# Storing three branches' gated terms apart and adding them in the last merge on VectorE

## Chip, cores and metric

The kernel runs on one core of one Trainium2 chip. The metric is device time in microseconds (us) of one execution; lower is better. Engines are named as in the profile: PE is TensorE (PEld its weight loads), DVE is VectorE, ACT is ScalarE, POOL is GpSimd, and SP (SyncE) issues most of the transfers.

## Reference

The program is a layer with four attention-like branches followed by a second block. The part that matters here is the merge of the four branches:

```python
branches = ((y_a, a_z), (y_b, b_z), (y_c, c_z), (y_d, d_z))
merged = None
for i, (y, z) in enumerate(branches):
    yi = y.reshape(B, S, BRANCH_W) * jax.nn.silu(z)
    term = jax.nn.sigmoid(h @ w_merge[i]) * (yi @ w_br[i])
    merged = term if merged is None else merged + term
return x + gate * (merged @ w_out)
```

With S = D = 1024 and BRANCH_W = 256, each term is a 1024 x 1024 matrix: a gate product of 1024 inner columns, a branch product of 256, and a sum of four such terms. Everything is in float32.

## The kernel before

All large products are computed transposed, in tiles of 128 x 512 (128 output columns of the model, 512 tokens, a "half"). A float32 product is three products of high and low halves (`mm3`, lines 229 to 231), so a gate tile is 24 matmuls of 512 columns and a branch tile is 6. `load_w` loads weights and splits them into a high half (ACT, or DVE at line 149) and a low half (line 155 on POOL or line 157 on DVE, in turn).

`merge(bi, y, step)` is called four times: step 0 for branch d, step 1 for branch a, step 2 for branch c, step 3 for branch b. Each has four groups of four tiles, 16 tiles in all. A group is put on the list `fillers` and issued by `fill`, which the attention loops of the next branch call between their tiles: step 1 runs beside branch c, step 2 beside branch b, step 3 after branch b's last tiles. In each step the running sum of the earlier steps lies in DRAM (`acc_d`), is loaded into `acc` (line 1134), gets the step's term added on POOL (line 1150) and is stored (line 1157); step 0 only stores, and step 3 keeps the result: ACT and DVE split it into `gT`, the left operand of the product with `w_out`.

The gate `tanh(x/2)` of six of the groups of `w_merge` is computed early, by `pre`, and stored in DRAM (`pre_d`): all four groups of branch a and two of branch c. For these, `w is None`, and the gate is loaded into `tz` (line 1137). Otherwise the tile computes it on PE and ACT (line 1142). The line that makes the term reads the gate and the PSUM bank of the branch product on DVE (line 1149): (gate + 1) x product. That instruction is what frees the bank. There are two banks with the tag `mm`, which gate products and branch products share in turn.

Buffers set the order of the work: `acc` and `tz` have two buffers each, `Pm` (tiles of 128 x 1024 in which the branches hold probabilities) has three, and weights have nine (`w`). A Tile scheduler orders the instructions of each engine by a simulated timeline, so a change of one instruction can move others. Every engine works through its own queue in order, SP's too: a transfer whose buffer is not free holds back those behind it.

Branch c (stick breaking) works per head: two sigmoids on ACT (lines 1101, 1102), two mask selects on POOL (line 1104), a scan on DVE (line 1106), a multiplication (line 1108) which alternates between DVE and POOL, transposes on PE (line 276), a split into high and low halves (`PT`, ACT and line 157 on DVE) and the product with the values on PE (line 816). Branch b is a banded softmax (`softmax_pair`, lines 838 to 860), whose results `y.put` and `gate` turn into the operand `y` of step 3.

Of the kernel before, what the change touches and what calls it, by code (L numbers as in the profile page):

```python
# [9 lines left out]
F32 = mybir.dt.float32  # L10
F32R = mybir.dt.float32r
AF = mybir.ActivationFunctionType
ALU = mybir.AluOpType
# [4 lines left out]
P = 128  # L18
# [58 lines left out]
def hybrid_then_mix_kernel(ctx: ExitStack, tc, I, c1, c2, out, dbg=None, upto=99):  # L77
    nc = tc.nc
    ve, ac, po, pe, sy = nc.vector, nc.scalar, nc.gpsimd, nc.tensor, nc.sync
# [7 lines left out]
    cur = [main]  # L87

    def nm(s):
        uid[0] += 1  # L90
        return f"{s}_{uid[0]}"
# [4 lines left out]
    def tmp(tag, n, bufs=2, dt=F32):  # L96
        return cur[0].tile([P, n], dt, name=nm(tag), tag=tag, bufs=bufs)
# [7 lines left out]
    def mmb():  # L105
        return bank("mm", _T["MM"])
# [77 lines left out]
    def load_w(srcs, n, kc=KC, per=None, tag="w", bufs=None, hieng=None, loeng=None, dma=None, order=None):  # L184

        per = per or min(kc, 1024 // n)
        w = W()
        w.h, w.l, w.per = {}, {}, per
        raws = []
        order = order or range(kc // per)  # L190
        for i, b in enumerate(order):
            raw = main.tile([P, per, n], F32, name=nm("wr"), tag=tag, bufs=bufs or NW)
            for src, c0 in srcs:
                (dma or sy).dma_start(raw[:, :, c0:c0 + src.shape[2]], src[:, b * per:(b + 1) * per, :])
            raws.append((b, raw))
            if len(raws) == _T["SG"] or i == len(order) - 1:
                split_w(w, raws, per, n, tag, bufs, hieng, loeng)
                raws = []
        w.hi = lambda k, c0, c1: w.h[k // per][:, k % per, c0:c1]
        w.lo = lambda k, c0, c1: w.l[k // per][:, k % per, c0:c1]  # L200
        return w

    def kview(ap):
        return ap.rearrange("(k p) n -> p k n", p=P)
# [59 lines left out]
    def gemm_T(dst, w, c0, a, half, ks=None):  # L264

        return mm3(dst, [(w.hi(k, c0, c0 + P), w.lo(k, c0, c0 + P), a.hi(k, half), a.lo(k, half))
                         for k in (ks or range(a.nk))])
# [232 lines left out]
    for kp in range(4):  # L500
# [18 lines left out]
        for q in range(4):  # L519
            w, c = first_w[q // 2], q % 2 * P  # L520
# [551 lines left out]
    def branch_c():  # L1072
# [20 lines left out]
        def tile_of(p, i, ops):  # L1093
# [3 lines left out]
            for hh in range(2):  # L1097
# [16 lines left out]
    acc_d = [[[dram.tile([P, 512], F32, name=f"acc{b}_{m}_{q}", tag=f"acc{b}_{m}_{q}", bufs=1) for q in range(2)]  # L1114
              for m in range(KC)] for b in range(3)]
    gT = A()

    def merge(bi, y, step):
        wm = kview(I["w_merge"][0, bi])
        wb = kview(I["w_br"][0, bi])  # L1120
        wbr = [None]

        def group(g):
            w = None
            if (bi, 2 * g, 0) not in pre_d:
                w = load_w([(wm[:, :, g * 256:(g + 1) * 256], 0)], 256)
            if g % 2 == 0:
                wbr[0] = load_w([(wb[:, :, g * 256:(g + 2) * 256], 0)], 512, kc=2, tag="w")
            for half in range(2):
                for m in range(2):  # L1130
                    k = 2 * g + m
                    acc = tmp("acc", 512)
                    if step:
                        sy.dma_start(acc[:], acc_d[step - 1][k][half][:])
                    t = tmp("tz", 512)
                    if w is None:
                        sy.dma_start(t[:], pre_d[bi, k, half][:])
                    else:
                        gp = mmb()
                        gemm_T(gp[:], w, m * P, hT, half)  # L1140
                        with stream(_T["STE"], -10000000):
                            ac.activation(t[:], gp[:], AF.Tanh, scale=0.5)
                    bp = mmb()
                    gemm_T(bp[:], wbr[0], (g % 2) * 256 + m * P, y, half)
                    with stream(_T["STE"], -10000000):
                        if step == 0:
                            ve.scalar_tensor_tensor(out=acc[:], in0=t[:], scalar=1.0, in1=bp[:], op0=ALU.add, op1=ALU.mult)
                        else:
                            ve.scalar_tensor_tensor(out=t[:], in0=t[:], scalar=1.0, in1=bp[:], op0=ALU.add, op1=ALU.mult)  # L1149
                            po.tensor_tensor(acc[:], t[:], acc[:], op=ALU.add)  # L1150
                        if step == 3:
                            if m == 0:
                                gT.alloc(half, g)
                            copy(gT.hi(k, half), acc[:], "a", 0.5)
                            sub_lo(gT.lo(k, half), acc[:], gT.hi(k, half), "v", 0.5)
                        else:
                            sy.dma_start(acc_d[step][k][half][:], acc[:])
        for g in range(4):
            fillers.append(lambda g=g: group(g))
# [185 lines left out]
    for m in range(2):  # L1345
        u, w, evac = conf_group(m)
# [21 lines left out]
    qk0, w, evac = qk_group(0)  # L1368
# [367 lines left out]
    for g in LED:  # L1736
# [4 lines left out]
        w = load_w([(w_up[:, :, g * P:(g + 1) * P], 0)], P)  # L1741
# [171 lines left out]
    acc = [ot(1024, 8, "acc") for _ in range(NT)]  # L1913
# [69 lines left out]
    for stage in range(2):  # L1983
        ts = {}
        for i, (sn, tn) in enumerate(order):
# [5 lines left out]
            for q in range(4):  # L1991
# [18 lines left out]
                if (stage, i, q) in tails:  # L2010
                    t = tails[stage, i, q]
# [93 lines left out]
```

## Time and profile before

| | |
|---|---|
| time, median of 3 runs | 2323.44 us (2321.71 to 2327.45) |
| the profiled execution's own time | 2326.04 us |
| its span in the trace | 2324.3 us |
| mean granted clock of PE | 0.989 |
| PE busy | 2235.5 us, 96% |
| DVE busy | 1518.4 us, 65% |
| ACT busy | 962.6 us, 41% |
| POOL busy | 495.1 us, 21% |

The trace is one execution. Busy time is the union of an engine's instructions; what stands in square brackets behind an instruction is the idle time of its engine just before it and whom it waited for. Matmuls are pipelined, so one takes longer than its share of the time. The granted clock is given as a share of PE's full 2.4 GHz; 0.5 is the lower level, 1.2 GHz.

### The profile page before, as it was taken

What the parts mean: (1) busy time and instruction counts of PE and PEld (TensorE: products, weight loads), DVE (VectorE), ACT (ScalarE), POOL (GpSimd) and SP (SyncE); (2) the same over time, 40 slices, a digit from 0 to 9 for tenths busy, and PEclk for the clock granted to TensorE, in tenths of its full rate; (3) what the DMA queues carried; (4) which work ended last, traced back from release to release, by engine and by line L of the source; (5) the groups of instructions that cost most, each with busy time, mean ns of one, the idle gap of its engine ahead of it and who ended that gap; (6) DMA issues with size and microseconds to landing.
All of it is one profiled execution on the core that took longest, in us unless ns stands there. A gap on an engine that the chain in (4) does not pass through costs nothing.

```text
span 2324.3 us, 30295 instructions
## 1 busy us (share of the span) xinstructions
PE 2235.5 (96%) x11004; PEld 1853.1 (80%) x11004; DVE 1518.4 (65%) x2952; ACT 962.6 (41%) x1937; POOL 495.1 (21%) x411
## 2 busy tenths in 40 slices
PE   7999999999989999999998998899999999999998
PEld 6788788888887778877887787677788888888877
DVE  7634466665677965634579876855576778678684
ACT  6211344444455544422322344634445454334452
POOL 4222100010155622224320000012043440000021
PEclk9999999999999999999999999999999999999999
DMA  9432221121132333224320211156555687524313
GB/s 326 154 95 63 60 69 50 49 88 60 33 109 85 115 121 105 73 82 147 107 68 26 82 54 34 37 172 206 161 186 187 197 324 252 181 91 155 117 55 118
DMA packets 202783, 272.72 MB, mean 117 GB/s; under 512 B 17086, under 2 KB 126214, under 8 KB 202634
## 3 DMA queue, kind: packets, MB, share of 16 engines
q1 hardware_dynamic: 194240, 257.95, 34.3%
q10 hardware_dynamic: 8394, 12.84, 1.8%
q8 instruction: 87, 1.43, 0.3%
q14 instruction: 62, 0.51, 0.1%
HBM read 199.43 MB, written 71.32 MB: 116 GB/s over the span
## 4 chain that ended last, share of the span: by engine, by line
PE 46%; DVE 6%; DMA 2%; ACT 1%; issue 1%; POOL 0%; SPq 0%; DVEq 0%; POOLq 0%; ACTq 0%
PE mm L230 6%; PE mm L231 6%; PE mm L229 6%; DVE blk L1334 2%; PE s L1676 2%; PE s L1675 2%; PE s L1674 2%; PE t L2020 1%; PE t L2021 1%; PE t L2019 1%; PE t L276 1%; PE mm L2020 1%; PE t L1676 1%; PE t L1675 1%; PE t L1674 1%; PE mm L2021 1%
## 5 line engine op out<-in xcount | busy, mean ns | idle before, releaser
L229 PE MATMUL mm<-blk,wh 128*128 128x512 f32 x1264 | 506.4, 401 | 12.7 <-DVE tz L1149 5.3
L230 PE MATMUL mm<-blk,wh 128*128 128x512 f32 x1264 | 502.1, 397 | 0.9 <-DVE blk L157 0.9
L231 PE MATMUL mm<-blk,wl 128*128 128x512 f32 x1264 | 501.0, 397 | 2.0 <-POOL wl L155 1.7
L229 PEld LDWEIGHTS mm<-blk,wh 128*128 128x128 f32 x1264 | 239.4, 189 | 65.1 <-DVE tz L1149 7.9
L231 PEld LDWEIGHTS mm<-blk,wl 128*128 128x128 f32 x1264 | 239.4, 189 | 52.4 <-POOL wl L155 2.1
L230 PEld LDWEIGHTS mm<-blk,wh 128*128 128x128 f32 x1264 | 239.5, 189 | 47.8 <-DVE blk L157 1.3
L155 POOL TENSOR_TENSOR wl<-wr,wh 128x1024 fp32r<-128x1024 f32 (+1 forms) x50 | 122.9, 2458 | 480.1 <-ACT wh L147 290.2
L229 PE MATMUL mm<-wh,blk 128*128 128x512 f32 (+3 forms) x544 | 197.0, 364 | 7.1 <-DVE wh L149 1.6
L231 PE MATMUL mm<-wh,blk 128*128 128x512 f32 (+3 forms) x544 | 194.3, 359 | 1.0 <-DVE blk L157 1.0
L157 DVE SCALAR_TENSOR_TENSOR wh<-blk,wh 128x1024 fp32r<-128x1024 f32 x116 | 138.6, 1221 | 66.9 <-issue 59.2
L147 ACT ACTIVATE wh<-blk 128x1024 fp32r<-128x1024 f32 x116 | 117.0, 1053 | 154.4 <-PE s L2020 84.5
L230 PE MATMUL mm<-wl,blk 128*128 128x512 f32 (+3 forms) x480 | 170.2, 355 | 9.5 <-DVE wl L157 9.1
L147 ACT ACTIVATE blk<-mm 64x512 fp32r<-64x512 f32 (+3 forms) x138 | 77.9, 569 | 172.0 <-PE mm L231 113.2
L147 ACT ACTIVATE PT<-t 128x512 fp32r<-128x512 f32 (+3 forms) x224 | 96.0, 460 | 118.2 <-PE o L816 65.9
L147 ACT ACTIVATE wh<-wr 128x1024 fp32r<-128x1024 f32 (+2 forms) x91 | 93.7, 1031 | 102.2 <-DMA wr<-in_w_in_dram 21.9
L157 DVE SCALAR_TENSOR_TENSOR PT<-t,PT 128x512 fp32r<-128x512 f32 (+3 forms) x224 | 111.0, 515 | 37.4 <-ACT PT L147 36.4
L309 POOL TENSOR_TENSOR sm<-sm,mhalf 128x1 f32<-128x1 f32 x64 | 38.8, 610 | 437.3 <-DVE sm L308 422.0
L229 PEld LDWEIGHTS mm<-wh,blk 128*128 128x128 f32 x544 | 103.3, 190 | 25.4 <-DVE wh L149 2.4
L231 PEld LDWEIGHTS mm<-wh,blk 128*128 128x128 f32 x544 | 103.4, 190 | 16.8 <-DVE blk L157 1.9
L230 PEld LDWEIGHTS mm<-wl,blk 128*128 128x128 f32 x480 | 91.7, 191 | 24.3 <-DVE wl L157 11.3
L157 DVE SCALAR_TENSOR_TENSOR wl<-wr,wh 128x1024 fp32r<-128x1024 f32 (+2 forms) x69 | 88.5, 1283 | 31.5 <-PE mm L230 14.0
L1150 POOL TENSOR_TENSOR acc<-tz,acc 128x512 f32<-128x512 f32 x48 | 67.8, 1416 | 132.2 <-DVE tz L1149 86.4
(364 smaller groups left out, 4851.5 us busy)
## 6 DMA issues: line engine op xcount, KB each, us to landing
acc<-acc SPq DMA_DIRECT2D x96, 256.0 KB, 2.6
wr<-in_w_merge_dram SPq DMA_DIRECT2D x32, 512.0 KB, 4.0
wu<-in_w_up_dram SPq DMA_DIRECT2D x32, 512.0 KB, 5.1
blk<-in_w_down_dram SPq DMA_DIRECT2D x32, 512.0 KB, 7.0
blk<-ss SPq DMA_DIRECT2D x32, 512.0 KB, 4.7
wr<-in_w_in_dram SPq DMA_DIRECT2D x27, 512.0 KB, 4.2
ss<-us SPq DMA_DIRECT2D x48, 256.0 KB, 2.3
blk<-sa SPq DMA_DIRECT2D x24, 512.0 KB, 4.3
```

Of the source, the lines that this page charges most:

```text
L147: return ac.activation(dst, src, AF.Copy, scale=1.0 if scale is None else scale)
L155: return po.tensor_tensor(lo, x, hi.bitcast(F32), op=ALU.subtract)
L157: return ve.scalar_tensor_tensor(out=lo, in0=x, scalar=scale, in1=hi.bitcast(F32), op0=ALU.mult, op1=ALU.subtract)
L229: pe.matmul(dst, sh, mh, start=(i == 0), stop=False)
L230: pe.matmul(dst, sh, ml, start=False, stop=False)
L231: last = pe.matmul(dst, sl, mh, start=False, stop=(i == n - 1))
L1150: po.tensor_tensor(acc[:], t[:], acc[:], op=ALU.add)
L1334: ve.scalar_tensor_tensor(out=acc[:, c:c1], in0=u[:, c - l:c1 - l], scalar=w, in1=acc[:, c:c1], op0=ALU.mult, op1=ALU.add)
L1674: pe.matmul(dst, wh, xh, start=first and k == 0, stop=False, skip_group_check=True)
L1675: pe.matmul(dst, wh, xl, start=False, stop=False, skip_group_check=True)
L1676: last = pe.matmul(dst, wl, xh, start=False, stop=k == 3, skip_group_check=True)
L2020: pe.matmul(d, sh[:, c, ts_], tl[:, c, :], start=False, stop=False)
```

## The change

Steps 0 to 2 no longer add anything: each stores its own term in `acc_d[step]`. Step 3 loads the three stored terms of a tile, the first two into the halves of one `Pm` buffer and the third into `acc`, adds them with two additions on DVE, and adds its own term with a third, also on DVE (POOL added before). In steps 1 and 2, a gate that was computed early is loaded straight into `acc` and multiplied there, so that `tz` isn't used. The number of transfers is the same: 48 loads and 48 stores of `acc_d`, but all loads now stand in step 3.

```diff
--- before.py
+++ after.py
@@ -1130,9 +1130,14 @@
                 for m in range(2):
                     k = 2 * g + m
                     acc = tmp("acc", 512)
-                    if step:
-                        sy.dma_start(acc[:], acc_d[step - 1][k][half][:])
-                    t = tmp("tz", 512)
+                    if step == 3:
+                        two = cur[0].tile([P, 1024], F32, name=nm("Pm"), tag="Pm", bufs=_T["PM"])
+                        for j in range(2):
+                            sy.dma_start(two[:, j * 512:(j + 1) * 512], acc_d[j][k][half][:])
+                        sy.dma_start(acc[:], acc_d[2][k][half][:])
+                        ve.tensor_tensor(two[:, :512], two[:, :512], two[:, 512:], op=ALU.add)
+                        ve.tensor_tensor(acc[:], two[:, :512], acc[:], op=ALU.add)
+                    t = acc if w is None and step < 3 else tmp("tz", 512)
                     if w is None:
                         sy.dma_start(t[:], pre_d[bi, k, half][:])
                     else:
@@ -1143,11 +1148,10 @@
                     bp = mmb()
                     gemm_T(bp[:], wbr[0], (g % 2) * 256 + m * P, y, half)
                     with stream(_T["STE"], -10000000):
-                        if step == 0:
-                            ve.scalar_tensor_tensor(out=acc[:], in0=t[:], scalar=1.0, in1=bp[:], op0=ALU.add, op1=ALU.mult)
-                        else:
-                            ve.scalar_tensor_tensor(out=t[:], in0=t[:], scalar=1.0, in1=bp[:], op0=ALU.add, op1=ALU.mult)
-                            po.tensor_tensor(acc[:], t[:], acc[:], op=ALU.add)
+                        x_ = t if step == 3 else acc
+                        ve.scalar_tensor_tensor(out=x_[:], in0=t[:], scalar=1.0, in1=bp[:], op0=ALU.add, op1=ALU.mult)
+                        if step == 3:
+                            ve.tensor_tensor(acc[:], t[:], acc[:], op=ALU.add)
                         if step == 3:
                             if m == 0:
                                 gT.alloc(half, g)
```

The order of the instructions moves with it. On POOL, in step 1 beside branch c (`wl` is a weight's low half, `Pm` a probability tile), there stood before:

```order
L155 TENSOR_TENSOR wl_7106<-wr_7099,wh_7105 128x1024
L1150 TENSOR_TENSOR acc_6647<-tz_6649,acc_6647 128x512
L155 TENSOR_TENSOR wl_7449<-wr_7446,wh_7448 128x1024
L1150 TENSOR_TENSOR acc_6661<-tz_6663,acc_6661 128x512
L1104 AFFINE_SELECT Pm_6797<-Pm_6797 128x128
L1150 TENSOR_TENSOR acc_6675<-tz_6677,acc_6675 128x512
L1104 AFFINE_SELECT Pm_6839<-Pm_6839 128x128
L1104 AFFINE_SELECT Pm_6840<-Pm_6840 128x128
L1108 TENSOR_TENSOR Pm_6840<-Pm_6840,Pm_6839 128x767
L1150 TENSOR_TENSOR acc_6689<-tz_6691,acc_6689 128x512
L1150 TENSOR_TENSOR acc_6703<-tz_6705,acc_6703 128x512
L1104 AFFINE_SELECT Pm_6877<-Pm_6877 128x128
```

And now, at the same place:

```order
L155 TENSOR_TENSOR wl_7082<-wr_7075,wh_7081 128x1024
L155 TENSOR_TENSOR wl_7425<-wr_7422,wh_7424 128x1024
L1104 AFFINE_SELECT Pm_6773<-Pm_6773 128x128
L1104 AFFINE_SELECT Pm_6815<-Pm_6815 128x128
L1104 AFFINE_SELECT Pm_6816<-Pm_6816 128x128
L1108 TENSOR_TENSOR Pm_6816<-Pm_6816,Pm_6815 128x767
L1104 AFFINE_SELECT Pm_6853<-Pm_6853 128x128
```

The additions are gone from between the selects and the multiplications; nothing took their place. On DVE, where branch b's last attention tile meets step 3's first tiles (L856, L858 and L150 are the tile's softmax, L826 and L827 join its output, PT is its transposed probabilities), before:

```order
L157 SCALAR_TENSOR_TENSOR PT_9397<-t_9394,PT_9397 128x2x128 [waits Activation_49]
L847 TENSOR_TENSOR sm_9421<-mx_9409,c_63 128x2 [waits DVE_49]
L856 TENSOR_TENSOR sm_9423<-sm_9423,sm_9426 128x2 [waits Activation_49]
L858 RECIPROCAL sm_9430<-sm_9423 128x2 [waits DVE_49]
L150 TENSOR_SCALAR Pm_9410<-Pm_9410,sm_9430 128x256 [waits DVE_49]
L150 TENSOR_SCALAR Pm_9415<-Pm_9415,sm_9430 128x256
L1149 SCALAR_TENSOR_TENSOR tz_9756<-tz_9756,mm_9783 128x512 [waits PE_49,Activation_49]
```

Now, with two additions and their waits for transfers ahead of the softmax, and more behind it:

```order
L1138 TENSOR_TENSOR Pm_9625<-Pm_9625 128x512 [waits DMAHW3_49,DMAHW2_49]
L1139 TENSOR_TENSOR acc_9624<-Pm_9625,acc_9624 128x512 [waits DMAHW4_49,DVE_49]
L856 TENSOR_TENSOR sm_9343<-sm_9343,sm_9346 128x2 [waits Activation_49]
L1154 TENSOR_TENSOR acc_9624<-tz_9631,acc_9624 128x512 [waits DVE_49]
L858 RECIPROCAL sm_9350<-sm_9343 128x2 [waits DVE_49]
L150 TENSOR_SCALAR Pm_9330<-Pm_9330,sm_9350 128x256 [waits DVE_49]
L150 TENSOR_SCALAR Pm_9335<-Pm_9335,sm_9350 128x256
L157 SCALAR_TENSOR_TENSOR blk_9668<-acc_9624,blk_9667 128x512 [waits Activation_49]
L826 TENSOR_REDUCE blk_8759<-o_9280 64x128 [waits Activation_49]
L1138 TENSOR_TENSOR Pm_9672<-Pm_9672 128x512 [waits DMAHW5_49,DMAHW4_49]
L1152 SCALAR_TENSOR_TENSOR tz_9678<-tz_9678,mm_9705 128x512 [waits PE_49]
```

The additions of a tile (L1138, L1139) stand well ahead of its gated product (L1152), among branch b's instructions; each waits for transfers. On SP, at the same place, there stands now (the waits for PE are for transposes out of branch b's `Pm` tiles):

```order
L194 DMA wr_9808<-in_w_merge_dram 128x4x256 [waits DMAHW5_49,DVE_49]
L194 DMA wr_9810<-in_w_merge_dram 128x4x256 [waits PE_49]
L1136 DMA Pm_9625<-acc_0_0_730 128x512 [waits DVE_49,PE_49]
L1136 DMA Pm_9625<-acc_0_0_746 128x512 [waits DMAHW3_49]
L1136 DMA Pm_9672<-acc_1_0_732 128x512 [waits DMAHW4_49,DMAHW3_49,DVE_49]
L1136 DMA Pm_9672<-acc_1_0_748 128x512
L1137 DMA acc_9716<-acc_0_1_763 128x512 [waits DVE_49]
L1136 DMA Pm_9717<-acc_0_1_731 128x512 [waits DMAHW7_49,PE_49]
```

The loads of the stored terms come in pairs into `Pm`, where before one load of the running sum stood for each tile.

On PE the products keep their number; the order shifts by some matmuls against branch b's last tile. Between that tile's transposes and its last product stood four matmuls of a gate product and three of a branch product; now all 24 of a gate product and three of a branch product stand there.

## Rows read from the trace of the kernel before

**Rows 1.** Page, busy time of each engine (us, share of the span, instructions)

```profile
PE 2235.5 (96%) x11004; PEld 1853.1 (80%) x11004; DVE 1518.4 (65%) x2952; ACT 962.6 (41%) x1937; POOL 495.1 (21%) x411
```

**Rows 2.** Engines' busy time by stage: us, then busy (instructions), granted clock, DMA share, GB/s

```profile
660.00:870.00 210.00, 191.23 (x988) 158.42 (x988) 161.91 (x252) 105.24 (x240) 106.01 (x93) 0.98 0.36 111
970.00:990.00 20.00, 19.09 (x92) 15.55 (x91) 11.67 (x24) 6.82 (x19) 5.41 (x3) 1.00 0.13 39
990.00:1080.00 90.00, 87.67 (x374) 70.84 (x373) 27.27 (x33) 22.94 (x33) 27.42 (x18) 0.98 0.30 92
1080.00:1100.00 20.00, 15.38 (x64) 11.57 (x63) 12.62 (x8) 3.37 (x5) 10.74 (x5) 1.00 0.66 234
```

**Rows 3.** Timeline of PE, matmuls that waited: start, us, what [idle before <-releaser]

```profile
681.77 0.63 PE L276 MATMUL t<-c,Pm 128*128 128x128 f32 x4 [1.63 <-DVE PT L157]
692.13 1.06 PE L816 MATMUL o<-PT,cst 128*128 128x256 f32 x4 [2.09 <-DVE PT L157]
753.37 0.55 PE L276 MATMUL t<-c,Pm 128*128 128x128 f32 x3 [1.88 <-DVE Pm L1108]
```

**Rows 4.** Waits of PE, 660 to 1100 us: total us, times, longest

```profile
PE mm L229 <- DVE tz L1149: 5.3, 7, 1.5
PE mm L231 <- POOL wl L155: 1.7, 1, 1.7
```

**Rows 5.** Timeline of POOL and DVE around those waits

```profile
678.92 1.77 DVE L1108 TENSOR_TENSOR Pm<-Pm,Pm 128x639 f32<-128x639 f32 x1
768.73 0.81 DVE L1108 TENSOR_TENSOR Pm<-Pm,Pm 128x639 f32<-128x639 f32 x1
...
685.68 2.58 POOL L1150 TENSOR_TENSOR acc<-tz,acc 128x512 f32<-128x512 f32 x2
688.20 2.29 POOL L1104 TENSOR_SCALAR_AFFINE_SELECT Pm<-Pm 128x128 f32<-128x128 f32 x2
688.64 1.76 DVE L1106 TENSOR_TENSOR_SCAN Pm<-Pm 128x768 f32<-128x768 f32 x1 [0.19 <-POOL Pm L1104]
...
751.01 1.90 POOL L1150 TENSOR_TENSOR acc<-tz,acc 128x512 f32<-128x512 f32 x1
751.95 1.37 DVE L1108 TENSOR_TENSOR Pm<-Pm,Pm 128x383 f32<-128x383 f32 x1
```

**Rows 6.** Windows of 10 us in which the granted clock fell

```profile
690.00:700.00 10.00, 7.91 (x34) 6.70 (x34) 8.98 (x11) 4.86 (x11) 6.70 (x6) 0.83 0.54 167
750.00:760.00 10.00, 7.38 (x27) 5.37 (x26) 9.59 (x14) 4.16 (x10) 9.37 (x11) 0.69 0.65 191
1020.00:1030.00 10.00, 8.29 (x30) 5.99 (x29) 3.72 (x3) 2.06 (x3) 3.77 (x3) 0.84 0.52 165
```

**Rows 7.** Page and groups by shape: adds of 128x512 on POOL and on DVE

```profile
L1150 POOL TENSOR_TENSOR acc<-tz,acc 128x512 f32<-128x512 f32 x48 | 67.8, 1416 | 132.2 <-DVE tz L1149 86.4
...
L1833 DVE TENSOR_TENSOR blk<-us,blk 128x512 f32<-128x512 f32 x10 | 14.4, 1438 | 3.5 <-ACT us L147 3.5
L1937 DVE TENSOR_TENSOR acc<-run,acc 128x512 f32<-128x512 f32 x12 | 7.8, 688 | 0.0
```

**Rows 8.** Timeline of PE and DVE at the entry of the last merge

```profile
971.00 0.60 PE L276 MATMUL t<-c,Pm 128*128 128x128 f32 x4
974.32 0.16 DVE L856 TENSOR_TENSOR sm<-sm,sm 128x2 f32<-128x2 f32 x1 [1.53 <-ACT sm L855]
979.74 0.60 PE L276 MATMUL t<-c,Pm 128*128 128x128 f32 x4
981.80 0.64 PE L816 MATMUL o<-PT,blk 128*128 128x256 f32 x4
986.36 2.65 DVE L157 SCALAR_TENSOR_TENSOR blk<-blk,blk 128x512 fp32r<-128x512 f32 x1 [0.15 <-ACT blk L147]
```

**Rows 9.** Source line 1134 (loads of the running sum), DMA to landing, last row

```profile
DMA to landing us min/median/max: 2.5/2.8/3.6
```

**Rows 10.** Timeline of POOL inside the last merge

```profile
1061.83 1.29 POOL L1150 TENSOR_TENSOR acc<-tz,acc 128x512 f32<-128x512 f32 x1 [9.65 <-DMA acc<-acc]
```

## Prediction

> **What bounds the kernel now.** I read the page first: PE is busy 96% of the span [rows 1], so a change pays only where PE waits, or where a wait goes away together with the slow clock behind it. The engines' busy time by stage shows where the merges meet such waits. Step 0 of the merge lies before 480 us and has none; steps 1 and 2 run from 670 to 970 us, step 3 from 966 to 1080. From 660 to 870 us, while branch c computes, PE works 191.23 of 210 us, so 18.8 us are idle, with DVE at 161.91 and POOL at 106.01 us. From 870 to 970 us PE is full. At the entry of step 3 it loses 0.9 us (19.09 of 20), in the body 2.3 (87.67 of 90), and in the 20 us behind it 4.6 (15.38) [rows 2]. The granted clock fell in three windows: 10 us at 0.83 and at 0.69 inside branch c, and at 0.84 inside step 3, which cost 1.7, 3.1 and 1.6 us; each has a PE wait in it or just ahead of it [rows 6]. So the change can reach at most 18.8 + 1.7 + 3.1 = 23.6 us in steps 1 and 2, and 2.3 + 1.6 = 3.9 us in the body of step 3.
>
> **Part A: steps 1 and 2 lose the add on POOL and the load of the running sum.** Of the 48 adds at 1416 ns on POOL [rows 7], 32 stand here. They sit in POOL's queue between branch c's mask selects (L1104) and half of its multiplications (L1108); the order above shows them gone. The waits of PE show what that costs. At 681.77 PE waited 1.63 us for DVE, whose multiplication L1108 of 640 columns had taken 1.77 us, against 0.81 for the same shape at 768.73 [rows 3, 5]: 0.96 us lost. At 692.13 it waited 2.09 us: a scan (L1106) had started at 688.64, after a select at 688.20 that was queued on POOL behind two adds of 2.58 us [rows 3, 5]; I take back one add, 1.3 us. At 753.37 it waited 1.88 us for an L1108 of 1.37 us that started at 751.95, while an add held POOL until 752.91 [rows 3, 5]: 0.96 us. Together 3.2 us.
>
> These rows show a DVE operation on two SBUF tiles growing by the time that a POOL add still runs. The Trainium skill (SBUF — State Buffer, Who interferes with whom) says that a VectorE instruction with two SBUF inputs and a GpSimd instruction that reads SBUF exclude each other, and that the second to issue is blocked until the first ends. By that rule the same holds for the new adds on DVE, so it speaks against the change in step 3 as much as for it here; by itself it would not change the sum, because POOL keeps only weight splits in step 3.
>
> Seven more waits, 5.3 us, are for the gated product's own instruction (L1149) [rows 4], which frees PE's bank late. Its gate now has a buffer that holds a load and a store; the old accumulator's buffer held a load, the add and a store. One step of the ring drops out and none is new, so a loss here is excluded; I take half, 2.6 us. Both clock dips here follow waits of PE; I take half of 4.8 us, 2.4. The sum is 8.2 us. DVE stays busy for 77% of the stretch and works in order, so some waits will reappear behind other instructions: I take 6 us of the 8.2. **A = -6**, bounds 0 (every wait returns elsewhere) and -12 (half of 23.6).
>
> The load that is left out, 256 KB landing in 2.8 us [rows 9], is worth nothing by itself: only POOL waited for it, and POOL's wait is already in A.
>
> **Part B: the entry of step 3.** Here the change adds a wait. The first two terms go into a buffer that branch b's last attention tiles still use (`Pm`, three buffers), and the sum of them is in DVE's order ahead of the last tile's softmax. By the rows of before: the transposes that free the first buffer ran at 971.00 for 0.60; two DMA issues (0.3 us each) and 2.8 to land give about 975.0; two adds of 0.69 end at 976.4. The instruction behind them (L856) started at 974.32 [rows 8, 9]: 2.1 us later, and 2.8 with the third add that stands there too. The next pair is loaded after the last tile's transposes (979.74) and stands ahead of the lower halves (L157) of the transposed probabilities, which that tile's last product on PE needs: transposes, loads and the adds there give some 5.6 us more. So that product (981.80) comes about 8.4 us later. What hides it: PE has a gate product of 24 matmuls and three more between those transposes and that product, 27 x 0.234 = 6.3 us (0.234 from 87.67 us over 374 matmuls [rows 2]), where it had seven, 1.6 us; the cover grows by 4.7 us. That leaves 3.7 us. After it, the branch's last lower half (986.36, 2.65 us [rows 8]) stands behind a weight split and one more add, some 1.9 us, and PE already lost 0.9 us there. The sum is 5.6 us, but the loads may land before the softmax is due, and the gate product can run on meanwhile; I take **B = +4**. The bounds are 0 (all behind PE's gate products) and +8, to which a clock dip like that at 1020 (1.6) may add itself.
>
> **Part C: the body of step 3.** 48 adds move to or are new on DVE. Each takes 688 ns when POOL is quiet and 1438 ns when POOL adds beside it [rows 7], so 33 to 69 us; I take 33, since POOL is nearly empty here. DVE has 90 - 27.27 = 62.7 us free [rows 2], and a tile is 30 matmuls, 7.0 us, against 3 x 0.69 for its adds: hidden. If that cover were gone, the 33 us would be on the path. The wait on the running sum changes engine: POOL once sat 9.65 us for that load [rows 10], and now DVE would. Queued behind it on DVE is the gated product of the current tile, which frees PE's bank; PE needs the bank only 24 matmuls (5.6 us) later. Against this the step between the product and ACT's copy shortens by 1416 - 688 = 0.7 us, so the buffer for the next load and the group's weights behind it in SP's order come sooner, which should shrink the 1.7 us wait for a weight half (L155) [rows 4] and the clock dip after it. **C = -1**, bounds -3.9 and +3. The transfers grow by 32 x 256 KB, 8.4 MB over about 100 us or 84 GB/s, on top of 92; the stage behind moved 234 GB/s [rows 2], so I cost them at nothing.
>
> **Part D: the exit.** In the 4.6 us that PE loses behind step 3, DVE is splitting w_out; its last add, 0.69, stands among those splits: **D = +0.7**, bounds 0 and +1.4.
>
> **Sum.** -6 + 4 - 1 + 0.7 = -2.3 us. The profiled execution took 2326.04 us (span 2324.3 and 1.7 around it), so 2323.7 in its own time. It lies 2.6 us above the median of 2323.44, inside the three runs' spread of 5.7 us; on the median the sum gives 2321.1, and I say 2321.
>
> **The rivals.** *Nothing is given back* (faster): the entry is hidden and A comes whole, -8 to -12, with C at -1 to -3; 2310 to 2315. For it: DVE is at 9.6 of 10 us in the window at 750 [rows 6], so each freed microsecond there counts, and the clock dips may vanish whole. Against: the entry's order. *DVE blocks at the entry* (slower): the two loads ahead of the softmax make PE wait the full 8 us plus 1.6 of clock, and A brings less than 3; 2329 to 2333. It decides if the loads of the second pair land after the 6.3 us of cover. For it: the DVE order; against: PE's longer cover. *The waits only move* (no change): branch c's DVE, at 77%, sets its pace whichever engine adds; A and B both within 1, so 2322 to 2324. *The adds lock POOL's splits out*: eight splits (L155) of the 18 POOL instructions of the body would each wait for an add, 0.69 us; only the one for which PE waits counts, with its dip up to 3; 2324. This exclusion is the rule of the Trainium skill (SBUF — State Buffer, Who interferes with whom) cited in part A.
>
> **How the numbers follow.** Chances: the forecast 0.42, nothing given back 0.27, blocked at the entry 0.17, waits only move 0.09, splits locked out 0.05. About 0.3%, 7 us, is what a measurement of this kernel tells from no change. Faster than 2316.5 are the second case and a little of the first: 0.29. Slower than 2330.4 is most of the third: 0.15. The rest, 0.56, is within. The forecast's own range is 2316 to 2327; the range that reaches into the neighbours is 2311 to 2331.
>
> **What would show it.** Right: from 660 to 870 us of the same work PE's idle time falls from 18.8 to 11 to 14 us, the mean L1108 on DVE gets shorter, and the window clock of 0.69 is gone or milder; at the entry DVE waits on a load of `Pm` or `acc` (L1138, L1139), and PE idles 3 to 6 us within 25 us; in the body no PE wait on L1152 above 1 us. Wrong: no wait of PE at the entry (then B is 0 and the time is near 2316 or below), or PE's idle time in branch c unchanged (A is 0, then 2325 or above), or adds on DVE nearer 1.4 us than 0.69 and PE waiting for L1152 in the body.

## The result

The changed kernel takes 2346.45 us (median of 4 runs, 2341.58 to 2352.42) against 2323.16 for the kernel before: a ratio of 1.0099, 95% interval 1.0082 to 1.0116, so about 23 us slower. The forecast was 2321, in a range up to 2331, with a chance of 0.15 for slower. The time lies outside that range, on the slower side.

### The profile page after: what moved, and what is told of

The parts are those of the page before. It is cut to its first block, busy times and chain, and to the rows that moved or that the text cites. A ratio compares the mean times of both kernels' runs of the same rounds, so it can differ in the third digit from the quotient of the medians.

```text
span 2342.5 us, 30253 instructions
## 1 busy us (share of the span) xinstructions
PE 2243.0 (96%) x11004; PEld 1858.8 (79%) x11004; DVE 1538.6 (66%) x3000; ACT 961.0 (41%) x1937; POOL 422.0 (18%) x363
## 4 chain that ended last, share of the span: by engine, by line
PE 78%; DVE 10%; DMA 4%; ACT 2%; issue 1%; POOL 1%; SPq 0%; DVEq 0%; POOLq 0%; ACTq 0%
PE mm L229 15%; PE mm L230 14%; PE mm L231 14%; PE t L276 3%; PE o L816 3%; DVE blk L1338 3%; PE s L1678 2%; PE s L1680 2%; PE s L1679 2%; PE t L2024 1%; PE t L2025 1%; PE t L2023 1%; PE mm L2024 1%; PE t L1678 1%; PE t L1680 1%
## 5 line engine op out<-in xcount | busy, mean ns | idle before, releaser
L229 PE MATMUL mm<-blk,wh 128*128 128x512 f32 x1264 | 508.6, 403 | 27.7 <-DVE acc L1152 12.3
L229 PEld LDWEIGHTS mm<-wh,blk 128*128 128x128 f32 x544 | 104.5, 193 | 23.8 <-DVE blk L149 2.1
L816 PE MATMUL o<-PT,blk 128*128 128x256 f32 x508 | 88.4, 295 | 2.5 <-DVE PT L157 2.4
```

The lines of the kernel that those rows point to most:

```text
L229: pe.matmul(dst, sh, mh, start=(i == 0), stop=False)
L816: behind_pe[0] = pe.matmul(dst, v(lo + c0 + j), PT[:, j].rearrange("p a q -> p (a q)"), start=start and c0 + j == 0, stop=stop and c0 + j ...
```

## The profile after

The page's busy times of the changed kernel, which answer to [rows 1]:

```profile
PE 2243.0 (96%) x11004; PEld 1858.8 (79%) x11004; DVE 1538.6 (66%) x3000; ACT 961.0 (41%) x1937; POOL 422.0 (18%) x363
```

POOL lost 73 us and DVE gained 20, as planned; PE's busy time grew by 7.5 us with the same number of matmuls, and the mean granted clock went from 0.989 to 0.986, so part of the loss is slower clock. Its profiled execution spans 2342.5 us, 18.2 more than before; the medians differ by 23, so some 5 us of the loss don't show in this pair of executions.

To see where the 18.2 went, I count matmuls. The windows view tells how many have started up to a time; both kernels have 11004. The windows begin at 0, so they give the moment at which the 3600th, 4950th and 5700th has started: near the beginning of step 1, just ahead of step 3, and behind its exit (between those ends the order differs, so a count there is a rough guide). The kernel before:

```profile
0.00:675.58 675.58, 656.94 (x3600) 558.16 (x3601) 393.14 (x1106) 274.14 (x628) 132.86 (x121) 0.99 0.29 93
0.00:960.91 960.91, 925.80 (x4950) 780.83 (x4951) 598.19 (x1513) 414.69 (x976) 254.33 (x223) 0.99 0.31 99
0.00:1138.80 1138.80, 1095.83 (x5700) 918.08 (x5700) 675.79 (x1632) 466.08 (x1082) 313.77 (x265) 0.99 0.31 100
```

The changed kernel:

```profile
0.00:674.46 674.46, 654.52 (x3600) 556.45 (x3601) 392.25 (x1106) 274.02 (x628) 131.00 (x120) 0.99 0.29 93
0.00:969.95 969.95, 926.17 (x4950) 781.76 (x4950) 591.13 (x1515) 413.92 (x977) 201.98 (x191) 0.99 0.28 89
0.00:1158.50 1158.50, 1101.94 (x5700) 921.38 (x5701) 696.64 (x1680) 465.20 (x1082) 241.47 (x217) 0.98 0.31 98
```

Steps 1 and 2 took 295.5 us instead of 285.3, so 10.2 were lost where 6 were to be gained; PE's idle time in them rose from 16.5 to 23.8. Step 3 with its exit took 188.6 instead of 177.9, a loss of 10.7 where 3.7 was forecast. The program's start (-1.1) and the rest (-1.5) make up the difference to 18.2.

The waits of PE from 640 to 1140 us of the changed kernel (total, times, longest) tell which instructions were late; these are the three largest. L1152 is now the gated product (L1149 in [rows 4]):

```profile
PE mm L229 <- DVE acc L1152: 12.3, 11, 2.9
PE mm L229 <- ACT blk L147: 4.7, 2, 4.0
PE s L797 <- DVE blk L157: 4.7, 2, 2.8
```

Seven waits for the product, 5.3 us, have become eleven of 12.3. The first two places below explain the first two rows.

**The ring of buffers.** The queue of SP from 640 to 970 us waits, among others, for these two things (L1142 loads a ready gate, L1161 stores a term):

```profile
SPq L1161 <- DVE acc L1152: 71.1, 16, 11.4
SPq L1142 <- DMA acc<-acc: 45.4, 19, 5.0
```

19 of the 24 gate loads wait for a transfer, the store of a term. The timeline shows one such turn, SP, DVE and PE together (start, duration):

```profile
759.03 0.67 DVE L1152 SCALAR_TENSOR_TENSOR acc<-acc,mm 128x512 f32<-128x512 f32 x1
759.99 0.42 SPq L1161 DMA_DIRECT2D acc<-acc  x1
763.28 0.32 SPq L1142 DMA_DIRECT2D acc<-pre  x1
768.54 0.69 DVE L1152 SCALAR_TENSOR_TENSOR acc<-acc,mm 128x512 f32<-128x512 f32 x1 [2.23 <-DMA acc<-pre]
769.28 0.50 PE L229 MATMUL mm<-blk,wh 128*128 128x512 f32 x1 [2.93 <-DVE acc L1152]
```

The product of 759.03 is stored at 759.99. The next gate can go into that buffer only when the store has landed, so its load is issued at 763.28, and the product that needs it starts at 768.54, with PE idle for 2.93 us. (This load is also the slowest of its kind, 5.2 us from issue to landing; the median of L1142 is 2.9.) Before, the gate's buffer came free when POOL had added it, and the store of the sum held another buffer. SP waited nearly as long for that store, but with the load of the running sum, which only POOL reads:

```profile
SPq L1134 <- DMA acc<-acc: 39.3, 26, 3.9
```

**The entry of step 3.** By the same count, these are the stretches from the 5000th to the 5150th matmul (the entry), on to the 5450th (the body) and on to the 5500th (the exit), of the kernel before and then of the changed one:

```profile
971.12:1005.00 33.88, 32.97 (x153) 26.97 (x152) 15.49 (x29) 10.86 (x25) 9.26 (x6) 1.00 0.23 71
1005.00:1078.41 73.41, 71.08 (x302) 57.26 (x301) 21.49 (x24) 17.82 (x26) 22.84 (x14) 0.98 0.27 84
1078.41:1095.41 17.00, 12.38 (x52) 9.15 (x51) 13.74 (x8) 4.45 (x7) 11.48 (x5) 1.00 0.83 295
979.93:1020.12 40.19, 36.16 (x152) 28.57 (x151) 28.07 (x45) 10.51 (x24) 4.05 (x2) 0.92 0.53 164
1020.12:1096.86 76.74, 72.06 (x302) 56.95 (x300) 39.21 (x52) 18.24 (x27) 8.24 (x4) 0.98 0.40 128
1096.86:1115.15 18.29, 14.22 (x52) 10.22 (x51) 10.53 (x9) 3.51 (x6) 12.62 (x5) 0.91 0.81 284
```

The entry takes 6.3 us longer, the body 3.3 and the exit 1.3. In the entry PE idles 3.1 us more and is busy 3.2 us longer, at a mean clock of 0.92. DVE, POOL, ACT and PE in the order of time:

```profile
994.36 2.41 POOL L155 TENSOR_TENSOR wl<-wr,wh 128x1024 fp32r<-128x1024 f32 x1 [29.48 <-PE mm L231]
994.41 0.41 DVE L826 TENSOR_REDUCE blk<-o 64x128 f32<-64x256 f32 x1
995.12 2.20 DVE L1138 TENSOR_TENSOR Pm<-Pm 128x512 f32<-128x512 f32 x1 [0.30 <-DMA Pm<-acc]
997.34 0.42 DVE L826 TENSOR_REDUCE blk<-o 64x128 f32<-64x256 f32 x1
997.79 0.69 DVE L1139 TENSOR_TENSOR acc<-Pm,acc 128x512 f32<-128x512 f32 x1
998.40 0.29 DVE L827 TENSOR_TENSOR blk<-blk,ju 128x128 f32<-128x128 f32 x1
998.77 1.64 POOL L620 TENSOR_TENSOR blk<-blk,tz 128x512 f32<-128x512 f32 x1 [2.00 <-DVE blk L827]
1000.44 0.63 ACT L147 ACTIVATE blk<-blk 128x512 fp32r<-128x512 f32 x1 [5.32 <-POOL blk L620]
1001.12 1.42 PE L229 MATMUL mm<-blk,wh 128*128 128x512 f32 x2 [4.03 <-ACT blk L147]
```

On DVE one addition of a later tile stands between the two reductions (L826) that join branch b's output, and another between them and the last instruction of the join (L827). The first took 2.20 us instead of 0.69, beside a weight split on POOL. POOL's gate (L620) and ACT's copy follow, and step 3's first products of that half need the copy. PE waits 4.03 us. The windows, which answer to [rows 6] and [rows 2], show the clock at this stall and at those of the body:

```profile
1000.00:1010.00 10.00, 8.88 (x27) 6.47 (x28) 6.65 (x9) 3.52 (x5) 0.41 (x1) 0.69 0.50 158
1060.00:1070.00 10.00, 7.00 (x25) 4.76 (x24) 5.66 (x7) 2.06 (x3) 1.75 (x1) 0.88 0.55 184
```

**The body of step 3.** The waits of DVE, then of ACT, from 990 to 1120 us:

```profile
DVE acc L1139 <- DMA acc<-acc: 20.1, 10, 2.9
DVE Pm L1138 <- DMA Pm<-acc: 14.2, 10, 2.2
```

```profile
ACT blk L147 <- DVE acc L1154: 46.7, 12, 7.3
```

A late load holds back DVE, where the gated product and weight splits stand behind the sums, and ACT, where the copy of the sum stands ahead of the next tile's tanh. (ACT waited before too, 34.7 us in 11 waits, for POOL's sum.) PE then waits for each:

```profile
1062.07 0.69 DVE L1139 TENSOR_TENSOR acc<-Pm,acc 128x512 f32<-128x512 f32 x1 [2.84 <-DMA acc<-acc]
1063.41 0.50 PE L229 MATMUL mm<-blk,wh 128*128 128x512 f32 x1 [0.65 <-DVE tz L1152]
1064.18 0.63 ACT L147 ACTIVATE blk<-acc 128x512 fp32r<-128x512 f32 x1 [7.24 <-DVE acc L1154]
1066.30 0.50 PE L229 MATMUL mm<-blk,wh 128*128 128x512 f32 x1 [1.22 <-ACT tz L1147]
1066.29 0.69 DVE L1138 TENSOR_TENSOR Pm<-Pm 128x512 f32<-128x512 f32 x1 [2.20 <-DMA Pm<-acc]
1068.17 0.79 PE L231 MATMUL mm<-blk,wl 128*128 128x512 f32 x1 [1.14 <-DVE wl L157]
```

These three waits of PE make 3.0 us within 5; in the whole body its idle time grew by 2.4. The clock fell there (the window from 1060 at 0.88 costs 1.2 us), but it had fallen once in the body before as well [rows 6], and its mean over the body is the same. In the exit PE idles no longer than before (4.1 us against 4.6), but its clock is 0.91 against 1.00, and why it fell there isn't shown.

## The experiments

The theory after the result has two causes that add up: the ring of two buffers in steps 1 and 2, and waits for loads at the wrong place of DVE's order in step 3. The rivals are the scheduler's new order alone, the `Pm` buffers, and the engine that adds. The table gives each kernel's median and ratio to the kernel before on the same chip, and by its profile the time that each part took more than before (start to matmul 3600, steps 1 and 2 to 4950, step 3 and exit to 5700, the rest).

| kernel | us | ratio (95%) | start | steps 1, 2 | step 3 | rest |
|---|---|---|---|---|---|---|
| changed | 2346.45 | 1.0099 (1.0082 to 1.0116) | -1.1 | +10.2 | +10.7 | -1.5 |
| e1_own_gate | 2331.39 | 1.0034 (1.0022 to 1.0045) | -4.6 | -3.6 | +13.2 | +0.3 |
| e2_ring4 | 2331.33 | 1.0031 (1.0020 to 1.0042) | +1.0 | -4.0 | +9.2 | -0.8 |
| e5_first_only | 2334.45 | 1.0046 (1.0031 to 1.0060) | -1.0 | +9.0 | -2.9 | +1.2 |
| e6_last_only | 2334.65 | 1.0048 (1.0033 to 1.0064) | -2.2 | +0.3 | +7.2 | +0.7 |
| e8_late_sum | 2335.83 | 1.0043 (1.0028 to 1.0058) | -1.2 | +10.0 | -2.5 | +3.4 |
| e3_pool_sum | 2344.22 | 1.0088 (1.0071 to 1.0106) | -2.5 | +12.4 | +5.9 | +1.6 |
| e9_own_late | 2314.75 | 0.9958 (0.9943 to 0.9973) | -3.0 | -1.9 | +0.1 | -7.9 |
| e9_again | 2317.06 | 0.9968 (0.9957 to 0.9979) | +0.1 | -1.6 | -0.3 | -8.4 |
| e10_two_in_3 | 2319.88 | 0.9984 (0.9973 to 0.9994) | +2.0 | -2.4 | -0.2 | -0.3 |
| e7_dve_chain | 2323.29 | 0.9992 (0.9981 to 1.0004) | +2.8 | +7.8 | -5.1 | -3.0 |
| e11_sum_in_2 | 2341.85 | 1.0073 (1.0058 to 1.0088) | +0.6 | +9.2 | -1.3 | +2.8 |

The start varies between -4.6 and +2.8 us; no edit touches it, and the kernel that ran twice has -3.0 and +0.1. The four parts come from one execution of each kernel. Those of e7_dve_chain (2328.70 us) and e10_two_in_3 (2325.17) took some 5 us more than their medians, that of e11_sum_in_2 (2337.30) some 5 less, so a part of 2 or 3 us that stands in one profile alone says little.

### The two parts apart

```diff
 e5_first_only (against the change)
                     if step == 3:
-                        two = ...
-                        for j in range(2): sy.dma_start(two[...], acc_d[j][k][half][:])
                         sy.dma_start(acc[:], acc_d[2][k][half][:])
-                        ve.tensor_tensor(two..., two..., two..., op=ALU.add)
-                        ve.tensor_tensor(acc[:], two[:, :512], acc[:], op=ALU.add)
...
-                            ve.tensor_tensor(acc[:], t[:], acc[:], op=ALU.add)
+                            po.tensor_tensor(acc[:], t[:], acc[:], op=ALU.add)

 e6_last_only: steps 0 to 2 as before, with running sum and POOL's addition; step 3 as in the change
```

> Steps 0 to 2 as in the change, step 3 as before: one load, the sum on POOL. The terms of steps 0 and 1 are left out of the result. It prices the change's first part alone. If the loss is made in steps 1 and 2 (9 us by the lag of PE's work) and 10 us more in step 3, this is 2330 to 2336 us. Rival, the whole loss comes with step 3: 2316 to 2324, the gain that the prediction gave to steps 1 and 2.

> Steps 0 to 2 as before (running sum, POOL's add), step 3 as in the change: three loads, three additions on DVE. The result counts the first terms more than once. It prices the change's last part alone: by the lag of PE's work 10 to 11 us, so 2331 to 2337 us. If step 3 costs only what the prediction gave it, 4 us: 2325 to 2329. If the costs of the two parts don't add up, since the order at one place decides the other, this and the kernel with the first part alone together differ from the whole loss of 23 us by more than 6.

Measured: 2334.45 and 2334.65 us, 10.6 and 10.8 above the kernel before. Together they give 21.4 of the whole loss of 23, so by the medians the parts are nearly independent. In the first, steps 1 and 2 lose 9.0 us and step 3 gains 2.9; in the second, steps 1 and 2 stay (+0.3) and step 3 loses 7.2. By the profiles step 3 doesn't add up so well: 7.2 and -2.9 stand against 10.7 in the change, though the first kernel's step 3 is that of before. So some of it depends on what steps 1 and 2 did, and why isn't shown. The second shows also the step that part B forecast, in the timeline of DVE and PE:

```profile
973.17 0.69 DVE L1138 TENSOR_TENSOR Pm<-Pm 128x512 f32<-128x512 f32 x1 [2.29 <-DMA Pm<-acc]
975.51 0.60 DVE L150 TENSOR_SCALAR Pm<-Pm,sm 128x256 f32<-128x256 f32 x2
975.90 0.76 PE L276 MATMUL t<-c,Pm 128*128 128x128 f32 x4 [2.49 <-DVE Pm L150]
```

DVE waits for a load ahead of branch b's softmax, whose last multiplication (L150) PE needs.

### The ring of buffers

```diff
 e1_own_gate
-                    t = acc if w is None and step < 3 else tmp("tz", 512)
+                    t = tmp("tz", 512)
 e2_ring4
-                    acc = tmp("acc", 512)
+                    acc = tmp("tz" if w is None and step < 3 and m else "acc", 512)
```

> The change with one part undone: in steps 1 and 2 the ready gate is loaded into its own buffer (two of them) again, and the gated product goes from there into the accumulator buffer that is stored. Theory of the ring: in place, a gate's load has to wait until the store of the tile two back has landed, so the gated product on DVE waits for its gate, and PE for the product (12.3 us in 11 waits between 640 and 1140 us after the change, 5.3 in 7 before). Then these waits fall to 6 us or less, the lag of PE's work against the kernel before at the end of step 2 falls from 9 us to between -2 and +3, and the time is 2334 to 2340 us. Rival, the loss in steps 1 and 2 comes from the new order of branch b's projections, which no buffer decides: waits for the product stay near 12 us or the lag stays near 9 us, 2343 to 2349.

> The change, still multiplied in place, but the ready gates of steps 1 and 2 go in turn into the two accumulator buffers and the two gate buffers, so that the ring has four places instead of two and needs no more memory. If the ring's depth is what costs, this does as well as the gate's own buffer: PE's waits for the gated product 6 us or less, 2334 to 2340 us. If multiplying in place costs by something else (the store reading what DVE has just written), the time stays at 2343 to 2349.

Measured: 2331.39 and 2331.33 us, so either repair gives back 15 us, rather more than expected. Steps 1 and 2 went from +10.2 to -3.6 and -4.0. The second still multiplies in place, with four buffers instead of two; so it's the ring's depth that costs, not the multiplication in place. Its gate loads still wait for stores (23.2 us in 13 waits of SP from 640 to 965 us), but early enough that PE waits only 0.7 us for the product. In the first, PE's waits from 640 to 1120 us are:

```profile
PE s L797 <- DVE blk L157: 5.3, 2, 4.0
PE mm L229 <- DVE acc L1152: 2.7, 3, 1.3
```

The waits for the product fell from 12.3 to 2.7 us. Its gate loads (SP's queue, 640 to 965 us) wait for instructions of POOL (37.6 us for L620, 11.2 for L1104), and none of their rows names a store any more.

The rival of the order is not empty: PE's 5.3 us of waiting for the projections that branch b's first scores (L797) need stand here as in the change (4.7), and before there was no such wait at that place. That the order cost them is likely, but not tried apart; steps 1 and 2 gain all the same.

### DVE's order in step 3

```diff
 e8_late_sum (e9_own_late: this and e1_own_gate)
-                        ve.tensor_tensor(two[:, :512], two[:, :512], two[:, 512:], op=ALU.add)
-                        ve.tensor_tensor(acc[:], two[:, :512], acc[:], op=ALU.add)
...
                         if step == 3:
+                            ve.tensor_tensor(t[:], t[:], two[:, :512], op=ALU.add)
+                            ve.tensor_tensor(t[:], t[:], two[:, 512:], op=ALU.add)
                             ve.tensor_tensor(acc[:], t[:], acc[:], op=ALU.add)
 e3_pool_sum: the first two additions of the change by po instead of ve
```

> The change with step 3's three additions made to follow the gated product (the two stored terms are added to the product, then the third), so that DVE meets none of their loads ahead of branch b's last softmax and its join; loads, buffers and the number of additions stay, and so do steps 0 to 2. Theory of DVE's order: the entry of step 3 costs 6 us in the change (9 in the kernel with the last part alone) since additions that wait for loads stand ahead of branch b's work on DVE. Then the lag over the entry falls to 0 to 3 us, and the time from 2346 to 2337 to 2342 us. Rival, the Pm buffers that step 3 takes from branch b are what costs: the entry's lag stays at 5 to 6 us, 2344 to 2349.

> The change with the two additions of stored terms in step 3 on POOL instead of DVE (the third stays on DVE). If DVE's in-order waits for the loads are what costs at the entry, this frees them: lag over the entry 0 to 3 us, 2337 to 2342 us. But POOL holds the weight splits and the gate of branch b, and its additions take 1.4 us instead of 0.7: by that rival the wait only changes engine, lag over the entry 5 us or more, 2343 to 2349.

Measured: 2335.83 us with the late sum. Loads, `Pm` buffers and the 48 additions are those of the change, and step 3 went from +10.7 to -2.5. DVE's waits for loads of stored terms, which were 20.1 and 14.2 us, are from 966 to 1090 us:

```profile
DVE acc L1154 <- DMA acc<-acc: 1.6, 1, 1.6
DVE tz L1152 <- DMA Pm<-acc: 0.4, 1, 0.4
```

(L1152 is here the first addition.) So here the buffers, the transfers and the number of additions cost nothing that shows; their place in DVE's order did. The -2.5 isn't a gain of theirs either: with the same steps 1 and 2 and the step 3 of before (e5_first_only) it is -2.9. On POOL the sum takes 2344.22 us, and step 3 loses 5.9. The wait changed its engine, as the rival had it:

```profile
994.58 3.00 POOL L1138 TENSOR_TENSOR Pm<-Pm 128x512 f32<-128x512 f32 x2
998.01 1.74 POOL L1139 TENSOR_TENSOR acc<-Pm,acc 128x512 f32<-128x512 f32 x1 [0.43 <-DMA acc<-acc]
999.71 1.28 POOL L620 TENSOR_TENSOR blk<-blk,tz 128x512 f32<-128x512 f32 x1
1001.70 0.51 PE L229 MATMUL mm<-blk,wh 128*128 128x512 f32 x1 [1.10 <-ACT blk L147]
```

Branch b's gate now stands behind the sums on POOL instead of behind those on DVE; PE waits 1.10 us for it, where it was 4.03.

### Both repairs, and two other ways to distribute the sum

```diff
 e10_two_in_3 (against the kernel before)
-                    if step:
-                        sy.dma_start(acc[:], acc_d[step - 1][k][half][:])
+                    if step > 1:
+                        sy.dma_start(acc[:], acc_d[2 * step - 4][k][half][:])
+                    if step == 3:
+                        one = cur[0].tile([P, 1024], F32, name=nm("Pm"), tag="Pm", bufs=_T["PM"])
+                        sy.dma_start(one[:, :512], acc_d[1][k][half][:])
...
-                        if step == 0:
+                        if step < 2:
...
+                            if step == 3:
+                                po.tensor_tensor(t[:], t[:], one[:, :512], op=ALU.add)
                             po.tensor_tensor(acc[:], t[:], acc[:], op=ALU.add)
 e11_sum_in_2: the same, but the second load and its addition (one in a tz buffer) in step 2
```

> Both repairs: the ready gate's own buffer in steps 1 and 2 (2331.4 us alone, 7.5 above the kernel before) and the late additions in step 3. If the two causes add up, 2321 to 2327 us, no slower than the kernel before. If the entry's cost is the buffers' or the transfers', 2329 to 2333.

> The kernel with both repairs once more, for a second profile. The first took 2314.75 us against 2325.5, but by its profile only 2 us of that lie in the merges: 3 lie at the program's start and 8 behind 1200 us, where nothing was changed but the order. If the part behind 1200 us is the order's, it is there again (6 to 9 us) and the time is 2312 to 2319; if it was that execution's, the lag behind 1200 us is within 3 us, and the time 2318 to 2324.

> The kernel before with another distribution of the sum: step 1 stores its term unadded, step 2, beside branch b, loads the terms of steps 0 and 1 and adds both on POOL, and step 3 is that of before, with one load and POOL's addition. It keeps what step 1 gave back with its own gate buffer (the lag of PE's work fell by 6 us beside branch c) and leaves step 3 alone. If POOL and the second load stay hidden beside branch b, where PE had no idle time: 2314 to 2320 us. If the second load's use of the gate buffers makes the gated products late there: 2322 to 2330.

> The kernel before with one load moved: step 1 stores its term unadded, step 2 loads and adds the term of step 0 on POOL, step 3 loads that sum and the term of step 1 (into a Pm buffer) and adds both on POOL behind the gated product. Step 1 should gain 6 us as with the gate's own buffer, the entry of step 3 cost 0 to 2 since nothing on DVE waits for a load, and step 2 stay as before: 2316 to 2322. If branch b's start loses time whenever step 1 is shortened (2 to 3 us with the gate's own buffer), 2320 to 2325.

Measured: with both repairs 2314.75 and 2317.06 us, faster than both kernels and than expected. The causes add up: steps 1 and 2 at -1.9 and -1.6, step 3 at +0.1 and -0.3. The entry still isn't free, though. In the first profile the scheduler put the late additions ahead of branch b's last softmax all the same, so DVE waits for a load there and PE for the softmax:

```profile
969.28 0.69 DVE L1152 TENSOR_TENSOR tz<-tz,Pm 128x512 f32<-128x512 f32 x1 [1.43 <-DMA Pm<-acc]
972.15 0.76 PE L276 MATMUL t<-c,Pm 128*128 128x128 f32 x4 [1.78 <-DVE Pm L150]
```

The other 8 us lie behind step 3, in both profiles, so they belong to the program and not to one execution. Nothing is edited there but the order of instructions; which one it is stays open. Without it the repaired change would be worth 2 us.

The sum in step 2 missed: 2341.85 us, with 9.2 us lost in steps 1 and 2, probably since two loads per tile share the two gate buffers there (not tried apart). Its trace agrees: beside branch b, PE waits 7.1 us in two places for the gated product, and ahead of the longer one DVE had waited 4.51 us for that gate's load. With one more load in step 3, the sum takes 2319.88 us, as expected; its profile has 2.4 us gained in steps 1 and 2, where 6 had been expected of step 1.

### The engine alone

```diff
 e7_dve_chain (against the kernel before)
-                            po.tensor_tensor(acc[:], t[:], acc[:], op=ALU.add)
+                            ve.tensor_tensor(acc[:], t[:], acc[:], op=ALU.add)
```

> The kernel before with nothing changed but the engine of the additions: all 48 go from POOL to DVE, in steps 1 to 3; running sum, loads, buffers as before. With the gate's own buffer and unadded terms, branch c's stretch gained 6 us. If it was POOL's additions that held up branch c's selects and multiplications, as part A of the prediction has it, that gain shows here too: lag from 670 to 826 us of the kernel before falls by 4 to 7 us, and the time is 2315 to 2321 us. If the gain came from the loads of the running sum that are left out, the lag there stays within 2 us: 2321 to 2327. If DVE can't take 48 more additions: above 2328.

Measured: 2323.29 us, no change that can be told. Steps 1 and 2 lose 7.8 us and step 3 gains 5.1. The multiplications on DVE did become shorter (row of line 1108, ns least, median, most; 294, 1026 and 3043 before):

```profile
L1108 DVE TENSOR_TENSOR Pm<-Pm,Pm x14: 292/808/1226, 654.3 to 817.1; 128x383 f32<-128x383 f32 x2, 128x511 f32<-128x511 f32 x2, 128x639 f32<-128x639 f32 x2, 128x767 f32<-128x767 f32 x2
```

But PE's waits from 640 to 870 us have this at their head:

```profile
PE mm L229 <- DVE tz L1149: 11.1, 8, 3.2
```

PE's waits for L1108 fell from 2.9 us to 0.5 in this stretch, as part A had it, but those for the gated product rose from 5.3 to 11.1: the additions on DVE delay the products instead. So it isn't enough to take the addition off POOL when DVE gets it.

## Why the prediction was wrong

**What bounds the kernel** was read rightly in the main: most of the losses and gains lie in waits that PE already had, together with windows of lower clock at the longest of them.

**Part A, -6, measured +10.2.** The step that failed is the sentence "one step of the ring drops out and none is new, so a loss here is excluded". I compared the lengths of two rings and not what the gated product waits for. Before, its gate lay in a ring that ended with POOL's addition, while the store kept only the sum's ring waiting, and there it was POOL that waited (16.6 us for that load from 640 to 970 us). In place, one ring holds both, and the gate's load waits for the store. With four buffers or a gate buffer of its own, steps 1 and 2 are at -4.0, -3.6, -1.9 and -1.6; so the sign that part A gave to leaving out the addition was right, its size a quarter to two thirds of the 6, and the ring cost 12 to 14 us on top. The rows behind A are borne out in one point: L1108 on DVE has a median of 888 ns in the change against 1026, and PE, which had waited 2.9 us for it, no longer does. That this time stays PE's is not borne out: in the kernel with DVE's additions other waits took it back.

**Part B, +4, measured +6.3, and 9.2 with the last part alone.** The place and the kind of wait were right, and the time lies within the bounds of 0 to 8, but the two terms were sized the wrong way round. The larger, 3.7 us for the softmax's delay, is not there in the change: the 4.7 us of additional cover by PE's gate products hid it, and PE has no wait for L150. It is there in the kernel with the last part alone (2.49 us). The smaller, 1.9 us for the join of branch b's output, was the one that decided: 4.03 us of PE's idle time against 0.91, and then a window at 0.69 of the clock, 3.1 us.

**Part C, -1, measured +3.3, just outside its bounds.** That 48 additions hide in DVE's free time was right: the late sum has them all, and step 3 is at -2.5, where that of before has -2.9 beside the same steps 1 and 2. The step that failed is "PE needs the bank only 24 matmuls (5.6 us) later". It looked at one wait of DVE alone. But ACT's copy waits for the same sum and stands ahead of the next gate's tanh, which frees the other bank, and a weight split stands behind the next sum, so PE waited 0.65, 1.22 and 1.14 us within 5 us. The ten waits of 2.0 us each on the third load were not in the sum at all; I had them as POOL's old wait changing its engine [rows 10], where the gated products did not stand behind them.

**Part D, +0.7, measured +1.3, within its bounds,** but not by the added instruction: PE idles there 0.6 us less than before and is busy 1.8 us longer, at the lower clock.

**The rivals.** The one on the other side, blocked at the entry, came nearest with its place and its 8 us and dip, but it too let A bring a gain. No case had steps 1 and 2 as a loss, so none could give 2346. *The adds lock POOL's splits out* counted eight splits among the 18 instructions of POOL in the body; there are four, and eight only up to 1100 us. It came the other way round: POOL's split of 2.41 us held an addition for 2.20 instead of 0.69. This agrees with the Trainium skill (SBUF — State Buffer, Who interferes with whom), by which the later of the two waits: the addition ended 0.55 us after the split.

## What to carry to other kernels

When a buffer is saved by working in place, ask whose wait is now in the chain: a load that had to wait for a compute instruction may now wait for a store to land, and two buffers that were enough for each of two rings may not be enough for one. Before additions are put on an engine with free time, see what stands behind them in its order; making them depend on something that is late anyway (here the gated product) is a way to set their place, though the scheduler may still put them ahead of other work, as with both repairs here. A sum of parts needs for each part a bound on the side of loss that is read from the rows, not excluded by an argument.

## What the runs showed of the hardware

A store in a ring counts with its time to land. Of the 48 stores of line 1161 in the changed kernel, least, median and most are:

```profile
DMA to landing us min/median/max: 2.0/2.2/5.4
```

In the kernel before they are 2.0, 2.1 and 4.3 us, so the change didn't slow the stores; it made a load wait for them that DVE and PE need.

And an edit in one step moved times some 100 to 500 us later in the program, where nothing was edited and only the order of instructions differs: -8 us in both profiles of the repaired kernel. In the other kernels that part lies between -3.0 and +3.4 us, by one profile each, which can be chance.
